# A list scheduler that knows PSUM banks, for a two-layer hybrid decoder trunk

## The chip, the cores and the metric

The kernel runs on one core of one Trainium2 chip. The metric is device time of one execution in microseconds (us). Three executions of the kernel before took 213.7, 214.15 and 214.66 us, with a median of 214.15.

## The reference

The reference takes a residual stream x of 256 rows by 1024 columns through two layers and a last RMSNorm, all in float32. Cut to what matters:

```
h = x
hn = rmsnorm(h, norm_gain[0])                      # layer 0: hn @ w_in (2832 columns)
  A: gated linear attention, 4 heads, chunks of 64, low-rank decay;  rmsnorm * silu(a_gate)
  B: sliding-window attention (128), 8 heads, 2 kv heads, sinks;     * silu(b_gate)
h = h + concat(A, B) @ w_out_even
hn = rmsnorm(h, norm_gain[1])                      # layer 1: hn @ w_in (2560 columns)
  C: causal attention over one block of 256, 8 heads, 2 kv heads;    * silu(c_gate)
h = h + C @ w_out_odd
out = h * rsqrt(mean(h * h) + 1e-6) * final_gain
```

With 256 rows there is one block of 256, so the block selection of branch C picks nothing and only a query's own causal block counts.

## The kernel before

The rows are two tiles (t = 0, 1) of 128; the 1024 model columns are eight tiles k of 128. Every large product is made of three fast matmuls: each operand is split into a rounded part ("h", as wh, xh, ogh) and a residual ("l", as wl, xl, ogl), and `products` (L381) adds h*h, l*h and h*l into one PSUM bank.

Weights come in chunks of 512 KB. `load_w` (L333) records for each chunk a DMA on SP's queue into one of four "raw" buffers, a rounding to wh (ScalarE or VectorE, whichever the planner picks) and a residual wl on VectorE. A fifth load has to wait until the raw buffer of the first has been read by both.

PSUM has eight banks of 128x512 float32: four "pj" for projections, two "s" for scores and transposes, one "t" for transposes, one "o" for attention outputs. `bank` (L317) hands them out in turn.

The work is first recorded and then issued. Each call on an engine goes through `Plan.record` (L156), which makes a node with its engine, a cost in ns, its dependences and the label of its section. `copy` (L75) makes a node that ScalarE or VectorE may do. `Plan.order` (L213) is a list scheduler: it keeps a clock for each engine, takes for each the candidate of the highest rank that is ready at the earliest time, and issues the one that starts first. A rank is the length of the path to the end plus numbers from the table `BOOST` (L278), one for each label and one for each label and engine. SP's loads keep the order in which they were recorded. Each engine then runs its list in that order, and semaphores keep the dependences.

Two places matter for the change. In the handover between the layers (L838 to L853) the residual sum h1 is made in five pieces (t = 0: two of 512 columns; t = 1: 512, 256, 256); each is transposed into an "s" bank in 128-wide blocks, and `split` (L376) turns every block into xh (a `copy`) and xl (VectorE, from the same bank and xh). In the tail (L907 to L932) the same five pieces of the last sum are added, squared and summed, multiplied by the final gain and scaled: the first piece of a tile is squared on ScalarE, the others on VectorE by one instruction that also adds to the sum so far; POOL takes the power -1/2; VectorE then scales 720 columns and ScalarE 304, and SP's and ScalarE's queues write them out.

Of the kernel before, what the change touches and what calls it, by code (L numbers as in the profile page):

```python
# [11 lines left out]
F32 = mybir.dt.float32  # L12
# [3 lines left out]
AF = mybir.ActivationFunctionType  # L16
# [33 lines left out]
class Plan:  # L50
# [12 lines left out]

    class Node:
        __slots__ = ("eng", "forms", "cost", "tail", "deps", "users", "path", "left", "ready", "end", "table", "dma", "idx", "load", "boost", "label",
                     "tag", "start", "rank")

    def __init__(self, nc):
        self.nodes, self.access, self.boost, self.label = [], {}, 0.0, "start"
# [86 lines left out]
    def record(self, eng, real, method, args, kw):  # L156
        if self.joined:
            node = self.joined[0]
            emit = node.forms[eng][2]
            node.forms = {eng: (node.cost, node.tail, lambda: (emit(), getattr(real, method)(*args, **kw)))}  # L160
            self.depend(node, args[:1], args[1:])
# [12 lines left out]
        node.boost = self.boost  # L174
        node.label = self.label
        (node.cost, node.tail), node.table, node.dma = self.cost(eng, method, out, args, kw), None, 0
        node.load = False
        node.forms = {eng: (node.cost, node.tail, lambda: getattr(real, method)(*args, **kw))}  # L178
        if eng == "ACT" and method == "activation":
            node.table = self.TABLE.get(args[2])  # L180
        if method == "dma_start":
            n = 4
            for _, c in list(out.ap):
                n *= c
            node.dma, node.load = n, "DRam" in type(args[1].tensor).__name__
        self.depend(node, outs, ins)

    def depend(self, node, outs, ins):
# [24 lines left out]
    def order(self):  # L213
# [8 lines left out]
        clock = dict.fromkeys(self.ENGINES, 800.0)  # L222
        cand = {e: [] for e in self.ENGINES}
        table, dma = None, 0.0
        for n in nodes:
            n.left, n.ready = len(n.deps), 0.0
            if not n.left:
                for e in n.forms:
                    cand[e].append(n)
        result, queue = [], [n.idx for n in nodes if n.eng == "SP"]  # L230
        while len(result) < len(nodes):
            best = None
            for e, c in cand.items():
                if e == "SP":
                    c = [n for n in c if n.idx == queue[0]] if queue else []
                if not c:
                    continue
                first = max(clock[e], min(n.ready for n in c))
                pick = max((n for n in c if n.ready <= first),
                           key=lambda n: n.rank - (PENALTY if n.table and n.table != table else 0))  # L240
                if best is None or (first, first + pick.forms[e][0]) < (best[0], best[0] + best[1].forms[best[2]][0]):
                    best = (first, pick, e)
            start, n, n.eng = best
            for e in n.forms:
                cand[e].remove(n)
            if n.eng == "SP":
                queue.pop(0)
            cost, tail, _ = n.forms[n.eng]
            if n.eng == "PE" and start < COLD:
                cost *= 1.85  # L250
            if n.table and n.table != table:
                table, cost = n.table, cost + 1283
            end = start + cost
            n.start = start
            clock[n.eng] = end
            if n.dma:
                dma = max(dma, start + (1500 if n.eng != "POOL" else 2500)) + n.dma / 400.0
                tail = dma + 500 + LATE - end
            result.append(n)
            for u in n.users:  # L260
                u.left -= 1
                u.ready = max(u.ready, end + 2 if u.eng == n.eng == "PE" else end + tail + self.latency(n, u))
                if not u.left:
                    for e in u.forms:
                        cand[e].append(u)
            n.end = end + tail
        self.span = max(n.end for n in nodes)
        return result

# [5 lines left out]
SIZE = {F32: 4, F32R: 4, BF16: 2, I8: 1}  # L275


BOOST = {"start": 98597, "start.DVE": 3254, "start.ACT": 96019, "start.PE": -31948, "rstd": 31475, "rstd.ACT": -37, "rstd.POOL": -24983, "rstd.PE": -12434, "bk": 36804, "bk.PE": 217, "bk.DVE": -81736, "bq": 3171, "bq.PE": 3109, "bq.DVE": -20905, "decay": 21203, "decay.PE": 74853, "decay.ACT": 3469, "decay.DVE": -187598, "bg": 11332, "bg.ACT": -33239, "bg.DVE": -731, "bg.PE": 899, "swa0": -12879, "swa0.PE": 10779, "swa0.POOL": -36260, "swa0.DVE": 45500, "swa0.ACT": 97090, "aq": -302768, "aq.ACT": -7847, "aq.DVE": -24230, "aq.PE": 7553, "ak": 6472, "ak.ACT": 904, "ak.DVE": -359375, "ak.PE": -179473, "swa1": -53249, "swa1.PE": 51429, "swa1.POOL": 127883, "swa1.DVE": -83638, "swa1.ACT": -185141, "gla": -44871, "gla.PE": 1809, "gla.ACT": 8127, "gla.DVE": 17088, "gla.POOL": -46, "ag": -382194, "ag.ACT": -117298, "ag.DVE": 4974, "ag.PE": -81161, "agate": 103853, "agate.ACT": -15208, "agate.PE": 106711, "oe": -565024, "oe.ACT": -6313, "oe.DVE": 33451, "oe.PE": -60361, "h1": -30627, "h1.DVE": 34676, "h1.PE": -40731, "h1.ACT": 94131, "h1.POOL": -72111, "odd": -133964, "odd.PE": 80018, "odd.DVE": -32828, "cv": 86415, "cv.DVE": -91321, "cv.PE": -14630, "ck": 5306, "ck.ACT": 54210, "ck.DVE": 16958, "ck.PE": -1368074, "q0": -42079, "q0.ACT": -37389, "q0.DVE": 81387, "q0.PE": -77423, "g0": 86994, "g0.ACT": 50548, "g0.DVE": 25243, "g0.PE": 146202, "moba0": 44850, "moba0.PE": 4255, "moba0.DVE": -5618, "moba0.ACT": 21294, "q1": -4528, "q1.ACT": -120247, "q1.DVE": 2101, "q1.PE": 54307, "g1": 25170, "g1.ACT": -104958, "g1.DVE": -60832, "g1.PE": -10042, "moba1": 165732, "moba1.PE": 38343, "moba1.ACT": -291161, "oo": -273149, "oo.ACT": -7130, "oo.DVE": -150278, "tail.DVE": 38832, "tail.ACT": -123887, "tail.POOL": -155413, "tail.SP": 30960}  # L278
COLD = 6500
WARM = 7  # L280
PENALTY, LATE = 12000, 600


@with_exitstack
def trunk(ctx: ExitStack, tc: tile.TileContext, t_in, out):
# [621 lines left out]
    nc.label = "tail"  # L907
    for t in range(NT):
        e = ends if t else (0, 512, D)
        y, r = xr[:, t], rstd[2][:, t:t + 1]  # L910
        total = buf("tot", [P, 1], F32, 4)
        for i, (lo, hi) in enumerate(zip(e, e[1:])):
            sl = slice(lo, hi)
            nc.vector.tensor_add(h1[:, t, sl], o[t, lo, hi], h1[:, t, sl])
            part_mean = ssq[:, 4 + 4 * t + i:5 + 4 * t + i]
            if i == 0:
                nc.scalar.activation(buf("junk", [P, D], BF16)[:, sl], h1[:, t, sl], AF.Square, scale=D ** -0.5,
                                     accum_out=part_mean)
# [77 lines left out]
```

## Time and profile before

The profiled execution is one further run, with the profiler's records.

| what | value |
|---|---|
| profiled execution's own time | 215.43 us |
| its span, first to last instruction | 213.7 us |
| median of three runs | 214.15 us |
| TensorE busy | 202.4 us, 95% |
| VectorE busy | 172.5 us, 81% |
| ScalarE busy | 109.3 us, 51% |
| GpSimd busy | 12.9 us, 6% |
| mean granted TensorE clock | 0.995 |
| read from HBM | 34.76 MB, 168 GB/s over the span |

A busy time is the sum of an engine's instructions, so overlaps with other engines are not taken off, and the ends of matmuls are modelled. The page also has a chain of work that ended last, followed back from the last instruction: 80% of it is TensorE, 6% VectorE, 5% DMA.

### The profile page before, as it was taken

What the parts mean: (1) busy time and instruction counts of PE and PEld (TensorE: products, weight loads), DVE (VectorE), ACT (ScalarE), POOL (GpSimd) and SP (SyncE); (2) the same over time, 40 slices, a digit from 0 to 9 for tenths busy, and PEclk for the clock granted to TensorE, in tenths of its full rate; (3) what the DMA queues carried; (4) which work ended last, traced back from release to release, by engine and by line L of the source; (5) the groups of instructions that cost most, each with busy time, mean ns of one, the idle gap of its engine ahead of it and who ended that gap; (6) DMA issues with size and microseconds to landing.
All of it is one profiled execution on the core that took longest, in us unless ns stands there. A gap on an engine that the chain in (4) does not pass through costs nothing.

```text
span 213.7 us, 3783 instructions
## 1 busy us (share of the span) xinstructions
PE 202.4 (95%) x1431; PEld 183.8 (86%) x1431; DVE 172.5 (81%) x358; ACT 109.3 (51%) x215; POOL 12.9 (6%) x38
## 2 busy tenths in 40 slices
PE   7899999999999999999898999999999999999970
PEld 3799999998898777888697999999999999888860
DVE  4699979998999998684578985876899998975662
ACT  3365857985998356611327500433868792613011
POOL 6005000010000000210001010000000000000101
PEclk9999999999999999999999999999999999999997
DMA  6999987673433094272027753157870019020022
GB/s 185 369 406 346 362 330 207 222 263 101 146 148 101 11 376 139 46 233 84 0 80 251 250 214 98 23 210 273 284 259 38 0 37 338 23 96 3 0 98 98
DMA packets 10913, 36.05 MB, mean 169 GB/s; under 512 B 1344, under 2 KB 2064, under 8 KB 10896
## 3 DMA queue, kind: packets, MB, share of 16 engines
q1 hardware_dynamic: 10464, 35.34, 48.0%
q10 hardware_dynamic: 432, 0.48, 0.6%
q8 instruction: 11, 0.18, 0.3%
q14 instruction: 6, 0.05, 0.1%
HBM read 34.76 MB, written 1.05 MB: 168 GB/s over the span
## 4 chain that ended last, share of the span: by engine, by line
PE 80%; DVE 6%; DMA 5%; issue 3%; ACT 2%; SPq 1%; POOL 0%; POOLq 0%; ACTq 0%; DVEq 0%
PE pj L178 61%; PE s L178 8%; PE o L178 7%; PE t L178 3%; DMA raw<-in_q 3%; DMA raw<-in_xav 3%; DVE xh L82 1%; PE s L160 1%; DVE xl L178 1%; DVE wl L178 1%; DVE wh L82 1%; ACT xh L178 1%; DVE xt L178 1%; SPq L178 1%; ACT wh L178 1%
## 5 line engine op out<-in xcount | busy, mean ns | idle before, releaser
L178 DVE TENSOR_TENSOR wl<-raw,wh 128x1024 fp32r<-128x1024 f32 (+2 forms) x59 | 68.5, 1170 | 2.9 <-ACT wh L178 1.8
L178 PE MATMUL pj<-xh,wh 128*128 128x256 f32 x224 | 54.9, 291 | 0.4 <-ACT wh L178 0.3
L178 PE MATMUL pj<-xh,wl 128*128 128x256 f32 x224 | 53.7, 288 | 0.0
L178 PE MATMUL pj<-xl,wh 128*128 128x256 f32 x224 | 53.6, 287 | 0.0
L178 ACT ACTIVATE wh<-raw 128x1024 fp32r<-128x1024 f32 (+2 forms) x36 | 36.5, 1016 | 32.3 <-PE pj L178 10.9
L178 PEld LDWEIGHTS pj<-xh,wh 128*128 128x128 f32 x224 | 38.5, 191 | 1.1 <-ACT wh L178 0.8
L178 PEld LDWEIGHTS pj<-xh,wl 128*128 128x128 f32 x224 | 38.4, 192 | 0.4 <-issue 0.3
L178 PEld LDWEIGHTS pj<-xl,wh 128*128 128x128 f32 x224 | 38.2, 191 | 0.2
L82 DVE CAST wh<-raw 128x1024 fp32r<-128x1024 f32 (+2 forms) x23 | 15.5, 672 | 16.9 <-PE pj L178 8.7
L178 PE MATMUL pj<-wl,ogh 128*128 128x512 f32 (+1 forms) x64 | 21.8, 376 | 0.0
L178 PE MATMUL pj<-wh,ogh 128*128 128x512 f32 (+1 forms) x64 | 21.6, 374 | 0.0
L178 PE MATMUL pj<-wh,ogl 128*128 128x512 f32 (+1 forms) x64 | 21.5, 374 | 0.0
L178 PE MATMUL pj<-wh,xl 128*128 128x328 f32 (+2 forms) x64 | 17.8, 348 | 1.9 <-DVE xl L178 1.9
L178 PE MATMUL pj<-wh,xh 128*128 128x328 f32 (+2 forms) x64 | 18.7, 357 | 0.7 <-ACT xh L178 0.4
L178 PE MATMUL pj<-wl,xh 128*128 128x328 f32 (+2 forms) x64 | 17.1, 333 | 0.0
L178 ACT ACTIVATE prob<-neg,mn 128x129 f32<-128x129 f32 (+3 forms) x32 | 14.2, 445 | 1.7 <-DVE mn L178 1.5
L178 PEld LDWEIGHTS pj<-wh,xl 128*128 128x128 f32 x64 | 11.6, 197 | 3.2 <-DVE xl L178 2.8
L178 PEld LDWEIGHTS pj<-wh,xh 128*128 128x128 f32 x64 | 11.5, 197 | 2.8 <-ACT xh L178 0.9
L178 PEld LDWEIGHTS pj<-wh,ogl 128*128 128x128 f32 x64 | 12.0, 189 | 1.9
L178 PEld LDWEIGHTS pj<-wl,ogh 128*128 128x128 f32 x64 | 11.9, 188 | 2.0 <-DVE wl L178 0.2
L178 PEld LDWEIGHTS pj<-wh,ogh 128*128 128x128 f32 x64 | 11.8, 188 | 1.8
L178 PE MATMUL t<-ident,prob 128*128 128x128 f32 x48 | 12.5, 276 | 0.0
(186 smaller groups left out, 338.1 us busy)
## 6 DMA issues: line engine op xcount, KB each, us to landing
raw<-in_oe SPq DMA_DIRECT2D x8, 512.0 KB, 4.2
raw<-in_q SPq DMA_DIRECT2D x8, 512.0 KB, 4.9
raw<-in_g SPq DMA_DIRECT2D x8, 512.0 KB, 4.5
raw<-in_oo SPq DMA_DIRECT2D x8, 512.0 KB, 4.2
raw<-in_bq SPq DMA_DIRECT2D x4, 512.0 KB, 6.4
raw<-in_bg SPq DMA_DIRECT2D x4, 512.0 KB, 5.5
raw<-in_ag SPq DMA_DIRECT2D x4, 512.0 KB, 3.8
raw<-in_xav SPq DMA_DIRECT2D x4, 456.0 KB, 6.5
```

The source lines that it names most:

```text
L82: lambda: getattr(self.vector._real, name)(*args, **kw))
L160: node.forms = {eng: (node.cost, node.tail, lambda: (emit(), getattr(real, method)(*args, **kw)))}
L178: node.forms = {eng: (node.cost, node.tail, lambda: getattr(real, method)(*args, **kw))}
```

## The change

Four things change. Each node gets a list of the PSUM banks it touches (`banks`). The scheduler's `order` remembers for every bank until when each engine uses it, and counts a node as ready only when the other engines' uses have ended (plus a hand-over latency). An engine other than SP may now be kept waiting for up to `LOOK` = 130 ns for a node whose rank is higher by more than `MARGIN` = 1500. The table `BOOST` has new numbers throughout. And the tail is written otherwise: every piece but a tile's last is squared on ScalarE and its sum added on by a one-column VectorE addition; only a tile's first 512 columns are multiplied by the gain ahead of the power, and the other 512 are multiplied by power and gain in one VectorE instruction; each output queue now takes 512 columns.

```diff
@@ record
+        node.banks = sorted({x.tensor.name for x in outs + ins if "PSUM" in str(getattr(x.tensor, "space", ""))})
@@ order
+        bank = {}
+
+        def ready(n, e):
+            return max([n.ready] + [t + self.latency(n, n) for b in n.banks for o, t in bank.get(b, {}).items() if o != e])
...
-                first = max(clock[e], min(n.ready for n in c))
-                pick = max((n for n in c if n.ready <= first),
-                           key=lambda n: n.rank - (PENALTY if n.table and n.table != table else 0))
+                when = {n.idx: ready(n, e) for n in c}
+                first = max(clock[e], min(when.values()))
+
+                def gain(n):
+                    return n.rank - (PENALTY if n.table and n.table != table else 0)
+
+                pick = max((n for n in c if when[n.idx] <= first), key=gain)
+
+                soon = [n for n in c if first < when[n.idx] <= first + LOOK and n.rank > gain(pick) + MARGIN]
+                if soon and e != "SP":
+                    pick = max(soon, key=lambda n: n.rank)
+                    first = when[pick.idx]
...
+            for b in n.banks:
+                bank.setdefault(b, {})[n.eng] = max(n.end, bank.get(b, {}).get(n.eng, 0.0))
@@ constants
-BOOST = {"start": 98597, "start.DVE": 3254, ...}
+BOOST = {"start": 308260, "start.DVE": -15127, ... "bq.DVE": -722225, ... "agate.DVE": -729706, ...}
-PENALTY, LATE = 12000, 600
+PENALTY, LATE, LOOK, MARGIN = 12000, 600, 130, 1500
@@ tail
-        y, r = xr[:, t], rstd[2][:, t:t + 1]
-        total = buf("tot", [P, 1], F32, 4)
+        y, r, mean = xr[:, t], rstd[2][:, t:t + 1], EPS
         for i, (lo, hi) in enumerate(zip(e, e[1:])):
             sl = slice(lo, hi)
             nc.vector.tensor_add(h1[:, t, sl], o[t, lo, hi], h1[:, t, sl])
             part_mean = ssq[:, 4 + 4 * t + i:5 + 4 * t + i]
-            if i == 0:
+            if hi < D:
                 nc.scalar.activation(buf("junk", [P, D], BF16)[:, sl], h1[:, t, sl], AF.Square, scale=D ** -0.5,
                                      accum_out=part_mean)
-                nc.vector.tensor_scalar(total, part_mean, EPS, None, op0=ALU.add)
+                total = buf("tot", [P, 1], F32, 4)
+                nc.vector.tensor_scalar(total, part_mean, mean, None, op0=ALU.add)
+                mean = total
             else:
                 nc.vector.tensor_tensor_reduce(out=buf("junk", [P, hi - lo]), in0=h1[:, t, sl], in1=h1[:, t, sl],
-                                               op0=ALU.mult, op1=ALU.add, scale=1.0 / D, scalar=total,
+                                               op0=ALU.mult, op1=ALU.add, scale=1.0 / D, scalar=mean,
                                                accum_out=part_mean)
-                total = part_mean
-            nc.boost = -2000.0
-            nc.vector.tensor_mul(y[:, sl], h1[:, t, sl], fg[lo // 512][:, lo % 512:hi - lo // 512 * 512])
-            nc.boost = 0.0
-        nc.gpsimd.tensor_tensor(r, total, half_neg[:, 0:1], op=ALU.pow)
-        nc.vector.tensor_scalar(y[:, 0:720], y[:, 0:720], r, None, op0=ALU.mult)
-        nc.sync.dma_start(out[t * P:(t + 1) * P, 0:720], y[:, 0:720])
-        nc.scalar.activation(y[:, 720:D], y[:, 720:D], AF.Copy, scale=r)
-        nc.scalar.dma_start(out[t * P:(t + 1) * P, 720:D], y[:, 720:D])
+            if i == 0:
+                nc.vector.tensor_mul(y[:, sl], h1[:, t, sl], fg[0])
+        nc.gpsimd.tensor_tensor(r, part_mean, half_neg[:, 0:1], op=ALU.pow)
+        nc.vector.scalar_tensor_tensor(y[:, 512:D], h1[:, t, 512:D], r, fg[1], op0=ALU.mult, op1=ALU.mult)
+        nc.sync.dma_start(out[t * P:(t + 1) * P, 512:D], y[:, 512:D])
+        nc.scalar.activation(y[:, 0:512], y[:, 0:512], AF.Copy, scale=r)
+        nc.scalar.dma_start(out[t * P:(t + 1) * P, 0:512], y[:, 0:512])
```

## Rows read from the trace of the kernel before

**Rows 1.** The page: busy us (share of span) x instructions of each engine.

```profile
PE 202.4 (95%) x1431; PEld 183.8 (86%) x1431; DVE 172.5 (81%) x358; ACT 109.3 (51%) x215; POOL 12.9 (6%) x38
```

**Rows 2.** Waits of TensorE (us in total, times, longest); last row 6 to 12 us.

```profile
PE pj L178 <- DVE xl L178: 1.9, 3, 0.7
...
PE o L178 <- ACT junk L178: 0.5, 1, 0.5
PE pj L178 <- ACT xh L178: 0.4, 1, 0.4
PE pj L178 <- ACT wh L178: 0.3, 1, 0.3
PE pj L178 <- DVE xt L178: 0.2, 1, 0.2
...
PE pj L178 <- DVE xl L178: 0.6, 1, 0.6
```

**Rows 3.** Timeline, 100 to 121 us: start, us, engine, operation, [idle before <-releaser].

```profile
101.61 0.37 ACT L178 ACTIVATE xh<-s,xt 128x128 fp32r<-128x128 f32 x1 [1.01 <-PE s L178]
...
102.02 0.35 DVE L82 TENSOR_SCALAR xh<-s,xt 128x128 fp32r<-128x128 f32 x1 [0.75 <-ACT xh L178]
...
103.07 1.12 DVE L178 SCALAR_TENSOR_TENSOR xl<-s,xt,xh 128x128 fp32r<-128x128 f32 x4
103.47 0.39 PE L178 MATMUL pj<-wh,xl 128*128 128x256 f32 x1 [0.58 <-DVE xl L178]
...
110.09 0.87 DVE L82 TENSOR_SCALAR xh<-s,xt 128x128 fp32r<-128x128 f32 x3 [0.38 <-ACT xh L178]
```

**Rows 4.** Waits of VectorE and of ScalarE for each other.

```profile
DVE xh L82 <- ACT xh L178: 2.3, 5, 0.8
...
ACT junk L178 <- DVE oa L82: 1.0, 1, 1.0
```

**Rows 5.** Chain of waits (start, us, what), 0 to 10 and 138 to 150 us.

```profile
7.79 0.84 DVE wl L178
...
139.83 1.14 DVE wl L178
...
141.37 6.16 DMA raw<-in_q
...
148.75 1.34 PE pj L178 x9
```

**Rows 6.** Timeline of the tail, 195 us to the end.

```profile
205.13 0.63 ACT L178 ACTIVATE junk<-xt 128x512 bf16<-128x512 f32 x1 [1.83 <-DVE xt L178]
...
205.67 0.19 ACT L178 ACTIVATION_READ_ACCUMULATOR junk<-xt 128x1 f32 x1
...
205.89 0.16 DVE L178 TENSOR_SCALAR tot<-ssq 128x1 f32<-128x1 f32 x1
...
206.86 0.28 PE L178 MATMUL o<-wl,ogh 128*128 128x256 f32 x1
207.05 0.48 DVE L178 CUSTOM_DVE_ANT_0 junk<-xt,tot 128x256 f32<-128x256 f32 x1
...
207.46 0.42 DVE L178 TENSOR_TENSOR xt<-o,xt 128x256 f32<-128x256 f32 x1
...
208.13 0.48 DVE L178 CUSTOM_DVE_ANT_0 junk<-xt,ssq 128x256 f32<-128x256 f32 x1
...
208.53 0.42 DVE L178 TENSOR_TENSOR xr<-xt,va 128x256 f32<-128x256 f32 x1
208.69 0.66 POOL L178 TENSOR_TENSOR rstd<-ssq,half_neg 128x1 f32<-128x1 f32 x1 [5.97 <-DVE ssq L178]
...
209.39 0.60 DVE L178 TENSOR_SCALAR xr<-xr,rstd 128x720 f32<-128x720 f32 x1 [0.44 <-POOL rstd L178]
```

**Rows 7.** Groups by form (xcount | busy us, mean ns | idle); last: POOL's timeline.

```profile
L178 DVE TENSOR_TENSOR wl<-raw,wh 128x1024 fp32r<-128x1024 f32 x53 | 64.2, 1220 | 2.8 <-ACT wh L178 1.8 <-PE pj L178 0.4
...
L178 DVE SCALAR_TENSOR_TENSOR ogl<-t,small,ogh 128x512 fp32r<-128x512 f32 x2 | 1.5, 748 | 0.4 <-ACT ogh L178 0.4
...
124.40 0.56 POOL L178 TENSOR_TENSOR rstd<-rsq,half_neg 128x1 f32<-128x1 f32 x1 [9.74 <-DVE rsq L178]
```

More of the change, by code (lines that the diff above doesn't have):

```diff
@@ L65 @@
         __slots__ = ("eng", "forms", "cost", "tail", "deps", "users", "path", "left", "ready", "end", "table", "dma", "idx", "load", "boost", "label",
-                     "tag", "start", "rank")
+                     "tag", "start", "rank", "banks")
     def __init__(self, nc):
@@ L160, in record @@
             node.forms = {eng: (node.cost, node.tail, lambda: (emit(), getattr(real, method)(*args, **kw)))}
+            node.banks = sorted({*node.banks, args[0].tensor.name})
             self.depend(node, args[:1], args[1:])
@@ L275 @@
 SIZE = {F32: 4, F32R: 4, BF16: 2, I8: 1}
-BOOST = {"start": 98597, "start.DVE": 3254, "start.ACT": 96019, "start.PE": -31948, "rstd": 31475, "rstd.ACT": -37, "rstd.POOL": -24983, "rstd.PE": -12434, "bk": 36804, "bk.PE": 217, "bk.DVE": -81736, "bq": 3171, "bq.PE": 3109, "bq.DVE": -20905, "decay": 21203, "decay.PE": 74853, "decay.ACT": 3469, "decay.DVE": -187598, "bg": 11332, "bg.ACT": -33239, "bg.DVE": -731, "bg.PE": 899, "swa0": -12879, "swa0.PE": 10779, "swa0.POOL": -36260, "swa0.DVE": 45500, "swa0.ACT": 97090, "aq": -302768, "aq.ACT": -7847, "aq.DVE": -24230, "aq.PE": 7553, "ak": 6472, "ak.ACT": 904, "ak.DVE": -359375, "ak.PE": -179473, "swa1": -53249, "swa1.PE": 51429, "swa1.POOL": 127883, "swa1.DVE": -83638, "swa1.ACT": -185141, "gla": -44871, "gla.PE": 1809, "gla.ACT": 8127, "gla.DVE": 17088, "gla.POOL": -46, "ag": -382194, "ag.ACT": -117298, "ag.DVE": 4974, "ag.PE": -81161, "agate": 103853, "agate.ACT": -15208, "agate.PE": 106711, "oe": -565024, "oe.ACT": -6313, "oe.DVE": 33451, "oe.PE": -60361, "h1": -30627, "h1.DVE": 34676, "h1.PE": -40731, "h1.ACT": 94131, "h1.POOL": -72111, "odd": -133964, "odd.PE": 80018, "odd.DVE": -32828, "cv": 86415, "cv.DVE": -91321, "cv.PE": -14630, "ck": 5306, "ck.ACT": 54210, "ck.DVE": 16958, "ck.PE": -1368074, "q0": -42079, "q0.ACT": -37389, "q0.DVE": 81387, "q0.PE": -77423, "g0": 86994, "g0.ACT": 50548, "g0.DVE": 25243, "g0.PE": 146202, "moba0": 44850, "moba0.PE": 4255, "moba0.DVE": -5618, "moba0.ACT": 21294, "q1": -4528, "q1.ACT": -120247, "q1.DVE": 2101, "q1.PE": 54307, "g1": 25170, "g1.ACT": -104958, "g1.DVE": -60832, "g1.PE": -10042, "moba1": 165732, "moba1.PE": 38343, "moba1.ACT": -291161, "oo": -273149, "oo.ACT": -7130, "oo.DVE": -150278, "tail.DVE": 38832, "tail.ACT": -123887, "tail.POOL": -155413, "tail.SP": 30960}
@@ new lines @@
+BOOST = {"start": 308260, "start.DVE": -15127, "start.POOL": 192, "start.ACT": 38547, "start.PE": -17663, "rstd": -19560, "rstd.ACT": 124955, "rstd.DVE": 115059, "rstd.POOL": -55563, "rstd.PE": -2940, "bk": 72927, "bk.PE": 5299, "bk.DVE": 11568, "bq": 7879, "bq.PE": -45059, "bq.DVE": -722225, "decay": 9816, "decay.PE": 6603, "decay.ACT": -500, "decay.DVE": 38759, "bg": -20668, "bg.ACT": 103347, "bg.DVE": 117872, "bg.PE": 64, "swa0": 19, "swa0.PE": -69516, "swa0.POOL": -109470, "swa0.DVE": -7370, "swa0.ACT": 282880, "aq": -181490, "aq.ACT": 4177, "aq.DVE": 60141, "aq.PE": 92879, "ak": 8425, "ak.ACT": -29078, "ak.DVE": -348491, "ak.PE": -362233, "swa1": -149581, "swa1.PE": -165615, "swa1.POOL": 19736, "swa1.DVE": 102002, "swa1.ACT": 306, "gla": -284590, "gla.PE": -120020, "gla.ACT": 42214, "gla.DVE": -71418, "ag": -374820, "ag.ACT": -22320, "ag.DVE": 335720, "ag.PE": -25022, "agate": 695074, "agate.ACT": 63820, "agate.DVE": -729706, "agate.PE": -71178, "oe": -546740, "oe.ACT": -89986, "oe.DVE": 195978, "oe.PE": 569, "h1": -81572, "h1.DVE": -112059, "h1.PE": 12477, "h1.ACT": -13693, "h1.POOL": 52549, "odd": 61629, "odd.PE": 41833, "odd.DVE": 22886, "cv": 183952, "cv.ACT": 16099, "cv.DVE": 16721, "cv.PE": -3543, "ck": -713826, "ck.ACT": 36419, "ck.DVE": 70132, "ck.PE": 92, "q0": 144341, "q0.ACT": -335824, "q0.DVE": 113390, "q0.PE": -39462, "g0": 15555, "g0.ACT": 29812, "g0.DVE": 4814, "g0.PE": -592, "moba0": -16830, "moba0.PE": 27130, "moba0.DVE": 310737, "moba0.ACT": 18881, "q1": 9659, "q1.ACT": -62076, "q1.DVE": -24498, "q1.PE": 767, "g1": 5202, "g1.ACT": 23863, "g1.DVE": -102820, "g1.PE": 3052, "moba1": -5391, "moba1.PE": 13736, "moba1.DVE": 5712, "moba1.ACT": -93948, "oo": -386614, "oo.ACT": 8440, "oo.PE": 16538, "tail": -83075, "tail.DVE": -60119, "tail.ACT": 22636, "tail.SP": 74670}
```

## The prediction, made before the changed kernel ran

> **What bounds the kernel now.** I read the page's busy times first [rows 1]. TensorE is busy for 202.4 us or 95% of the span, VectorE for 172.5 and ScalarE for 109.3. TensorE therefore sets the time: a new order of work can win only what TensorE loses in the fill at the start, between its matmuls, and behind its last one.
>
> Second, the waits of TensorE [rows 2], which are what an order can remove. They add up to 3.3 us: 1.9 for a residual part xl of the normalized operand (three times), 0.5 for a square on ScalarE, 0.4 for a rounded part xh, 0.3 for rounded weights wh, 0.2 for the residual stream. The same view of 6 to 12 us has one of the waits for xl, 0.6, and the wait for xh, 0.4: those are the fill. The other two waits for xl (0.58 at 103.47 [rows 3] and the longest, 0.7; together 1.3) are in the handover from layer one to layer two.
>
> Third, what stands before those waits, in order of time [rows 3]. Four pieces of one transposed bank "s" are rounded to xh, one on ScalarE at 101.61, the next on VectorE at 102.02, and so on by turns. They read different columns and write different columns, yet VectorE's piece has an idle 0.75 us before it that ends with ScalarE's piece. The list of waits says how much of that there is [rows 4]: VectorE waits 2.3 us in 5 places for ScalarE's xh. ScalarE's square of the branch output also waits 1.0 us for VectorE's scaled copy of the same bank, though neither needs the other's result. So two engines never read a PSUM bank together here, and the old planner, which knows no such rule, handed alternate pieces to two engines as if they ran side by side. This is the error that the change corrects.
>
> Behind TensorE's last matmul lie 6.6 us [rows 6]: it ends at 207.14 (206.86 and 0.28), the span at 213.7.
>
> **The change part by part.**
>
> *Bank knowledge.* It adds no instruction; it changes the times that the planner reckons with, and so who takes a piece and when. Price of the alternation: from the first xh at 101.61 to the start of the residuals at 103.07 are 1.46 us for four pieces [rows 3]. The same work on one engine: three pieces on VectorE took 0.87 us, so a further piece costs (0.87 - 0.35) / 2 = 0.26, and four take 0.35 + 3 x 0.26 = 1.13. That saves 0.33 us in each chain that alternates. The two handover waits of 1.3 us hang on such chains. Lower bound 0.66 (the faster chain alone), upper 1.3 (the planner, which now sees the chain at its true length, also places enough other matmuls beside it). I take 1.0, between the two, since TensorE has matmuls of both layers on hand at this point (the output product of one, the first projection of the next) and the planner can see that it lacks 0.3 us more.
>
> The 0.5 us behind the square: the two reads of the bank stay in line whoever does them, so the wait goes only if other matmuls are put there. Between 0 and 0.5; I take 0.2, nearer the lower end because the reads don't shorten.
>
> The remaining 0.3 for wh and 0.2 for the residual stream come from a DMA's landing and an addition, on which bank knowledge has no hold: 0. The fill: its 0.6 and 0.4 may shrink or grow by about as much when the start gets new priorities (the first chain runs through a DMA that no priority hastens): 0, with 0.6 either way.
>
> *Short looks ahead.* An engine may now stand idle for up to 130 ns when clearly more urgent work is about to be ready. SP is excepted. Queued behind the work so preferred is whatever else the engine had ready, a weight split above all, whose residual takes 1.22 us on VectorE [rows 7]. VectorE is idle for 41 us in all (213.7 - 172.5), so 0.13 us at a time is covered unless it falls where a split is late; I take 0, with the bad end in the rival below.
>
> *New priorities.* These reorder everything, and no row prices them directly. Bounds: a gain of at most what TensorE waits, 3.3 us; a loss of one or two late weight splits, priced below. I take 0 beyond the terms above.
>
> *Final scaling.* Before, after the last matmul [rows 6]: VectorE sums the squares of piece two (207.05, 0.48), only then adds piece three (207.46, 0.42, although TensorE was done at 207.14), multiplies piece two by the gain, sums piece three's squares (208.13), POOL takes the power (208.69, 0.66), VectorE scales 720 columns (209.39, 0.60), and 3.71 us after the end of that scaling (209.99) the span is over. After: piece two's squares go to ScalarE, and the gain of the upper half moves into the last scaling. VectorE is then free at 207.05, so the addition of piece three can start at 207.2 and end at 207.6. The sum that its square-sum needs is now a chain ScalarE to VectorE: for the 512-wide piece the square started at 205.13, its sum was out at 205.86 (205.67 and 0.19), and the one-column addition ended at 206.05 (205.89 and 0.16) [rows 6]: 0.92 us, the upper bound for 256 columns, so 207.05 + 0.92 = 207.97. With the 128-wide ScalarE piece's 0.37 [rows 3] in place of the 512-wide square's 0.63 it is 207.71, the lower bound. I take 207.85 for the square-sum's start, between the two as 256 lies between 128 and 512, 0.28 before 208.13: the wait for ScalarE takes the place of the removed multiplication, and wins a little.
>
> The power: 0.66 with a VectorE multiplication of two SBUF operands running beside it at 208.53, 0.56 alone, in the layer before [rows 6, 7]. After the change nothing of VectorE runs beside it: 0.10 gained. The Trainium skill (SBUF — State Buffer, Who interferes with whom) says that a VectorE instruction with two SBUF inputs contends with a GpSimd instruction that reads SBUF. The trace agrees with it by these two durations; without that rule the 0.10 would be chance, and the tail's gain 0.13 in place of 0.23.
>
> The last scaling now multiplies by a column and a second tensor: the nearest row, 128x512 with a column and a second tensor, took 0.748 against 0.60 for the 720 columns [rows 6, 7]: a loss of 0.15. ScalarE's part grows from 304 to 512 columns, by the square of that width 0.63 [rows 6], so it ends before VectorE does. The two output DMAs carry the same bytes in all, split evenly; they overlap already, so 0.
>
> Tail: 0.28 + 0.10 - 0.15 = 0.23 gained; between 0 and 0.5, as the last square is early or late.
>
> *Sum.* 1.0 + 0.2 + 0.23 = 1.4 us. The profiled execution took 215.43 us (span 213.7 and 1.7 around it), 1.28 above the median of the runs, 214.15. So 214.0 on the profiled execution's scale, and 212.7 as a median.
>
> **The rivals.**
>
> *More than the handover gains.* With a true picture of the banks, the new priorities also remove the waits that I left: all 3.3 us and the tail's 0.23, or 214.15 - 3.5 = 210.6. For: none of the waits is in TensorE's own work, and the fill's chain puts a weight residual of 0.84 us [rows 5] ahead of the operand that TensorE waits for, which an order can turn round. Against: the fill and the wait for wh hang on DMAs.
>
> *No change.* The banks' turns remain, since one bank is read by one engine at a time whatever the planner knows; if the handover has no more matmuls to put beside the chain, its waits move to a neighbouring place and only the tail's gain shows: 213.9. For: 95% of the span is TensorE's work, which stays. Against: the four xh alone are 0.33 us shorter on one engine, twice.
>
> *Slower: a weight split comes late.* SP issues loads in a fixed order, each when a raw buffer is free, that is, after the split of the chunk four earlier. In the chain of waits a residual runs at 139.83; after its end at 140.97 come SP's issue, a DMA of 6.16 us and a rounding on ScalarE, and TensorE starts at 148.75, having waited for that rounding [rows 2, 5]: 7.8 us from split to matmul, with nothing to spare. New priorities that put such a split behind one more residual and one 512-wide product of VectorE (1.22 + 0.75 [rows 7]) delay TensorE by 2.0 there. It decides as soon as a split ends less than 7.8 us before its buffer's next chunk is due. One such place, with the handover unimproved and the tail's gain, gives 214.15 + 2.0 - 0.23 = 215.9. For: the split labels' priorities are moved by hundreds of thousands, more than the length of the whole kernel in ns, so the paths' lengths alone no longer keep them in order. Against: the planner counts loads and buffers, so it sees most of this.
>
> That the change doesn't do what it says would be seen as an xh chain that still alternates; its time is that of no change.
>
> **How the numbers follow.** The forecast, 212.7, has 0.40; the larger gain, 210.6, 0.21; no change, 213.9, 0.23; slower, 215.9, 0.16. Within 0.5% (213.1 to 215.2) is about what a measurement of this kernel can't tell from no change. Faster: the first two, 0.40 + 0.21 = 0.61; same 0.23; slower 0.16. The forecast's own range, by the lower and upper terms (0.66 + 0 + 0 and 1.3 + 0.5 + 0.5, and half of the fill's 0.6 either way), is 211.5 to 213.8. For eight in ten the range reaches down to the larger gain and up to the edge of the slower case: 210.2 to 215.5.
>
> **What would show it.** Right: the wait of VectorE's xh for ScalarE's xh falls from 2.3 to under 0.5 us; TensorE's waits for xl after 10 us fall under 0.4; TensorE's last matmul ends at about 206.0 on the profiled scale; the last square-sum starts 0.7 us after TensorE's end in place of 1.0; the power takes about 0.56, the last scaling 0.75. Wrong: the handover's waits return as waits for another operand, or waits for wh or wl of over 1 us appear. A span in which TensorE ends earlier by more than 2 us would mean that the waits listed here were not all that the order cost.

## The result, and the profile after

The changed kernel takes 215.85 us (median of 17 runs, 214.8 to 217.49). The kernel before took 214.54 in 17 runs beside them. The ratio is 1.007, with a 95% interval of 1.0049 to 1.0091: slower by 0.7%, and outside the predicted range.

The profiled execution of the changed kernel took 217.33 us with a span of 215.6. That is 1.5 above its own median, where the profiled execution of before lies 0.9 above its own (215.43 against 214.54), so 0.6 of the 1.9 us between the two spans is scatter of single executions.

The page's line of busy times comes first, as in [rows 1].

```profile
PE 204.9 (95%) x1431; PEld 183.2 (85%) x1431; DVE 174.0 (81%) x358; ACT 111.4 (52%) x215; POOL 13.8 (6%) x38
```

TensorE runs the same 1431 matmuls as before, yet is busy for 204.9 us in place of 202.4. The overlap of one matmul with the next is counted once in this number (before, a matmul of 512 columns is listed with 0.39 us while the next starts 0.23 us after it, at 99.57 and 99.80), so a row of matmuls that is broken up by short stalls appears here as a busier engine. Next, the waits of TensorE, which answer to [rows 2] (us in total, times, longest; a wait for the warm-up at the start, the same in every kernel here, is left out).

```profile
...
PE s L179 <- DVE xt L179: 0.9, 1, 0.9
PE pj L179 <- DVE xl L179: 0.6, 1, 0.6
PE o L179 <- ACT ad L179: 0.6, 1, 0.6
PE pj L179 <- ACT wh L179: 0.3, 1, 0.3
PE o L179 <- DVE pTh L82: 0.3, 1, 0.3
```

The two handover waits for xl are gone: the 0.6 that is left is the fill. In their place stands one wait of 0.9 for the residual stream xt. The list is even shorter than before, 2.7 us against 3.3, and still TensorE ends at 209.35 in place of 207.14: the list alone would have given the wrong sign.

VectorE's waits (same columns) show what changed for it. The wait of its own xh pieces for ScalarE's, 2.3 us [rows 4], is not there any more. What it waits 1.9 us for, once, is a bank whose four xh ScalarE has all made, and which its residual xl needs. Its residuals wl now wait 7.3 us for the rounded weights, where they waited 1.8 [rows 7].

```profile
DVE wl L179 <- ACT wh L179: 7.3, 6, 2.0
...
DVE xl L179 <- ACT xh L179: 1.9, 1, 1.9
```

The timeline of the handover, 100 to 106 us, answers to [rows 3] (start, us, engine, operation, idle before and its releaser).

```profile
100.25 1.06 ACT L179 ACTIVATE wh<-raw 128x1024 fp32r<-128x1024 f32 x1 [4.31 <-DMA raw<-in_cv]
...
101.34 1.22 DVE L179 TENSOR_TENSOR wl<-raw,wh 128x1024 fp32r<-128x1024 f32 x1 [2.04 <-ACT wh L179]
...
102.48 0.74 DVE L179 SCALAR_TENSOR_TENSOR ogl<-t,small,ogh 128x512 fp32r<-128x512 f32 x1
...
103.15 1.21 DVE L179 TENSOR_TENSOR wl<-raw,wh 128x1024 fp32r<-128x1024 f32 x1
...
104.28 0.68 DVE L179 TENSOR_TENSOR xt<-pj,xr 128x512 f32<-128x512 f32 x1
...
105.02 0.66 PE L179 MATMUL s<-ident,xt 128*128 128x128 f32 x4 [0.87 <-DVE xt L179]
```

VectorE stands idle for 2.04 us at the head of its queue, with a residual whose weight chunk of branch C has landed late. Behind it in the same queue wait a residual of the gated output (ogl), one more weight residual and only then the first addition of h1, for whose transposes TensorE is waiting.

The chain of waits (start, us, what) shows the same place and the one that the slower rival had named [rows 5].

```profile
89.14 2.28 DVE wl L179 x2
...
92.85 7.32 DMA raw<-in_cv
100.25 1.07 ACT wh L179
...
104.36 0.61 DVE xt L179
105.02 0.66 PE s L179 x4
...
140.94 1.24 DVE wl L179
142.57 6.48 DMA raw<-in_q
149.16 1.07 ACT wh L179
150.27 1.22 PE pj L179 x8
```

By the page, VectorE now holds 20% of this chain and DMAs 15%, where it was 6% and 5% before; TensorE holds 52% in place of 80%. At 140 to 150 us the chain of [rows 5] runs as before. The chunk that lands late is one of in_cv, whose loads left SP from 92.85 on, behind two residuals of VectorE. Before, they left from 89.10 on:

```profile
89.10 0.85 SPq L178 DMA_DIRECT2D raw<-in_cv  x2
```

Last, the tail, which answers to [rows 6] (timeline, 208.4 us to the end).

```profile
208.43 0.42 ACT L179 ACTIVATE junk<-xt 128x256 bf16<-128x256 f32 x1 [1.77 <-DVE xt L179]
...
209.07 0.28 PE L179 MATMUL o<-wl,ogh 128*128 128x256 f32 x1
209.39 0.42 DVE L179 TENSOR_TENSOR xt<-o,xt 128x256 f32<-128x256 f32 x1 [0.20 <-PE o L179]
209.85 0.48 DVE L179 CUSTOM_DVE_ANT_0 junk<-xt,tot 128x256 f32<-128x256 f32 x1
...
210.42 0.54 POOL L179 TENSOR_TENSOR rstd<-ssq,half_neg 128x1 f32<-128x1 f32 x1 [7.29 <-DVE ssq L179]
...
211.00 0.75 DVE L179 SCALAR_TENSOR_TENSOR xr<-xt,rstd,va 128x512 f32<-128x512 f32 x1 [0.66 <-POOL rstd L179]
```

TensorE is done at 209.35 (209.07 and 0.28) and the span at 215.6: 6.25 us, against 6.56 before (213.7 - 207.14).

### The profile page after: what moved, and what is told of

Same layout as the page of the kernel before. It is cut to its first block, busy times and chain, and to the rows that moved or that the text cites. A ratio compares the mean times of both kernels' runs of the same rounds, so it can differ in the third digit from the quotient of the medians.

```text
span 215.6 us, 3774 instructions
## 1 busy us (share of the span) xinstructions
PE 204.9 (95%) x1431; PEld 183.2 (85%) x1431; DVE 174.0 (81%) x358; ACT 111.4 (52%) x215; POOL 13.8 (6%) x38
## 4 chain that ended last, share of the span: by engine, by line
PE 52%; DVE 20%; DMA 15%; issue 5%; ACT 4%; SPq 1%; POOL 1%; POOLq 0%; ACTq 0%; DVEq 0%
PE pj L179 40%; DVE wl L179 7%; PE s L179 5%; PE o L179 4%; DMA xr<-in_xr 4%; DMA raw<-in_cv 3%; DMA raw<-in_q 3%; DMA raw<-in_bq 3%; PE t L179 2%; DVE neg L179 2%; DVE og L179 2%; ACT wh L179 1%; ACT prob L179 1%; DMA raw<-in_av 1%; DVE am L179 1%
## 5 line engine op out<-in xcount | busy, mean ns | idle before, releaser
L179 PE MATMUL pj<-xh,wh 128*128 128x256 f32 x224 | 56.6, 289 | 0.3 <-ACT wh L179 0.3
L179 ACT ACTIVATE wh<-raw 128x1024 fp32r<-128x1024 f32 (+2 forms) x38 | 38.6, 1017 | 34.5 <-DMA raw<-in_q 11.6
L179 PE MATMUL pj<-xh,wl 128*128 128x256 f32 x224 | 55.7, 287 | 0.0
L179 PE MATMUL pj<-xl,wh 128*128 128x256 f32 x224 | 55.4, 286 | 0.0
L179 PEld LDWEIGHTS pj<-xh,wh 128*128 128x128 f32 x224 | 39.5, 191 | 1.3 <-ACT wh L179 0.7
L179 PEld LDWEIGHTS pj<-xh,wl 128*128 128x128 f32 x224 | 39.4, 191 | 0.7 <-DVE wl L179 0.2
L179 PEld LDWEIGHTS pj<-xl,wh 128*128 128x128 f32 x224 | 39.3, 191 | 0.1
L82 DVE CAST wh<-raw 128x1024 fp32r<-128x1024 f32 (+2 forms) x21 | 14.0, 666 | 15.4 <-PE pj L179 3.4
L179 PE MATMUL pj<-wh,ogl 128*128 128x512 f32 (+1 forms) x64 | 22.9, 372 | 0.0
L179 PE MATMUL pj<-wh,xh 128*128 128x328 f32 (+2 forms) x64 | 17.6, 342 | 0.1
```

Of the source, the lines that this page charges most:

```text
L82: lambda: getattr(self.vector._real, name)(*args, **kw))
```

## The experiments

Each ratio is to the kernel before, run beside it on the same chip, with its 95% interval. "Old table" means the numbers of `BOOST` before, "banks" the bank knowledge, "look" the short looks ahead.

**The tail by itself, put in and taken out.** tail_only is the kernel before with the new tail; tail_undone is the changed kernel with the old one.

```diff
-        nc.vector.tensor_scalar(y[:, 0:720], y[:, 0:720], r, None, op0=ALU.mult)
+        nc.vector.scalar_tensor_tensor(y[:, 512:D], h1[:, t, 512:D], r, fg[1], op0=ALU.mult, op1=ALU.mult)
...
```

> The old planner with its old priorities, and only the new tail. Theory (the loss lies in the new order of work, the tail gains): TensorE's end stays within 0.3 us of before's 207.1, the stretch behind it shrinks from 6.58 to about 6.25 us, as in the changed kernel, so 0.3 us faster than before, ratio about 0.9985. Rival (the new tail is the loss): over 1 us slower than before.

> The changed kernel with the old tail put back. Theory: 0.3 us slower than the changed kernel, so about 1.6 us slower than before (ratio about 1.008), with TensorE's end at about 209.3. Rival (the tail is the loss): back to before's time.

tail_only: 214.4 us, 0.9974 (0.9954 to 0.9994), a gain of 0.1 to 1.0 us. tail_undone: 216.02 us, 1.0044 (1.0019 to 1.007), which can't be told from the changed kernel's 1.007. Neither expectation came true as written: in tail_only's profile TensorE ends at 206.03, 1.1 us earlier than before and not within 0.3, and tail_undone is not slower than the changed kernel. The traces show why. With the old order the stretch behind TensorE shrinks from 6.56 to 6.37 us (212.4 - 206.03). With the changed kernel's order the old tail already needs only 6.13 (214.2 - 208.07), less than the new one's 6.25. TensorE's last matmul and the last square-sum of tail_undone are:

```profile
207.79 0.28 PE L179 MATMUL o<-wl,ogh 128*128 128x256 f32 x1
...
208.57 0.48 DVE L179 CUSTOM_DVE_ANT_0 junk<-xt,ssq 128x256 f32<-128x256 f32 x1
```

So the tail is worth a few tenths with the old order and shows no gain with the new one, and it is not what made the changed kernel slower.

**The banks by themselves, and the alternation by itself.** bank_only has the new `ready` and the new `banks`, with the old table, the old tail and no look (first fence, as against the changed kernel; its table and tail are those of before). xh_one_engine replays the order of before from a written list and only gives the alternating xh pieces to VectorE (second fence, shortened: in the code the list is packed).

```diff
-PENALTY, LATE, LOOK, MARGIN = 12000, 600, 130, 1500
+PENALTY, LATE, LOOK, MARGIN = 12000, 600, -1, 1500
```

```diff
-        for n in self.order():
-            n.forms[n.eng][2]()
+        for i, e in WRITTEN:
+            self.nodes[i].forms[e][2]()
```

> Old priorities, old tail, no look ahead; the scheduler only learns the banks. Theory of the prediction, first half (bank knowledge gains at the handover): the alternating xh go to one engine in pairs, VectorE's waits for ScalarE's xh fall from 2.3 to under 0.5 us, TensorE's handover waits for xl from 1.3 to 0.6 or less, and the time by 0.7 to 1.3 us (ratio 0.994 to 0.997). Rival (the chain was hidden or its waits only move): within 0.3 us of before. Second rival (bank knowledge makes the order worse, as in the changed kernel): over 0.5 us slower.

> Before's order, written down and replayed instruction by instruction, with one difference: the eight xh pieces of the first bank of each row tile in the handover, which alternate between ScalarE and VectorE, all go to VectorE. Theory: each of the two chains is 0.33 us or more shorter and TensorE's two waits for xl (0.58 and 0.7) shrink by about that, 0.4 to 0.9 us faster in all. Rival (other work on VectorE takes the gain back, since VectorE now has four more pieces of 0.35 us): within 0.3 us of before.

bank_only: 212.09 us, 0.986 (0.9831 to 0.989), 3.0 us faster and more than either theory gave. xh_one_engine: 213.86 us, 0.995 (0.9932 to 0.9969), 1.1 us faster (0.7 to 1.5), within the 0.66 to 1.3 that the prediction had worked out for the handover and a little over the 0.4 to 0.9 expected of this run. TensorE runs the same list here as before, so its two handover waits can be set side by side: they fall from 0.58 [rows 3] and 0.69 (first line) to 0.18 and 0.28, by 0.8 us in all.

```profile
116.12 0.39 PE L178 MATMUL pj<-wh,xl 128*128 128x256 f32 x1 [0.69 <-DVE xl L178]
```

```profile
102.37 0.39 PE L181 MATMUL pj<-wh,xl 128*128 128x256 f32 x1 [0.18 <-DVE xl L181]
...
114.70 0.39 PE L181 MATMUL pj<-wh,xl 128*128 128x256 f32 x1 [0.28 <-DVE xl L181]
```

The other 1.9 us of bank_only are left for all else that the planner arranges anew; no run takes them apart. The timelines of the handover show how the xh are now done: ScalarE takes all four in bank_only (first fence), VectorE in xh_one_engine (second).

```profile
101.15 1.14 ACT L179 ACTIVATE xh<-s,xt 128x128 fp32r<-128x128 f32 x4 [1.00 <-PE s L179]
```

```profile
100.94 1.12 DVE L85 TENSOR_SCALAR xh<-s,xt 128x128 fp32r<-128x128 f32 x4 [0.35 <-PE s L181]
```

Four pieces take 1.12 to 1.14 us on one engine (1.13 by the prediction), and 1.46 by turns [rows 3]. The Trainium skill (PSUM — Partial Sum Buffer, PSUM bank collisions raise a hardware error) asks software to guard PSUM by bank, reads against reads too; the idle 0.75 us of [rows 3] and its going away agree.

**Each new part taken out of the changed kernel.** numbers_undone has the old table, look_off no look, bank_off ignores the banks.

```diff
# bank_off
-            return max([n.ready] + [t + self.latency(n, n) for b in n.banks for o, t in bank.get(b, {}).items() if o != e])
+            return n.ready
```

> The changed kernel with the old priority table alone put back; banks, look ahead and tail stay new. Theory (the old table was fitted to a scheduler without a look; a look of 130 ns reorders its close decisions): clearly slower than the changed kernel, by several us, ratio to before 1.02 or more, so that the new table repairs what the look breaks. Rival (the new table by itself is the loss): about as fast as bank knowledge with the new tail, ratio about 0.984.

> The changed kernel with the look ahead alone switched off; banks, new table and tail stay. Theory (the new table is fitted to the look): slower than the changed kernel by 1 to 3 us, ratio to before 1.012 to 1.022. Rival (the look is the loss, whatever the table): faster than the changed kernel, at or under before's time.

> The changed kernel with bank knowledge alone switched off; look, new table and tail stay. Theory (bank knowledge is a gain wherever it stands): slower than the changed kernel by 2 to 5 us, ratio to before over 1.016, and VectorE again waits over 1 us for ScalarE's reads of the same bank. Rival (the bank rule is over-careful with this table): no slower than the changed kernel.

numbers_undone: 226.23 us, 1.0536 (1.0503 to 1.0568). look_off: 222.4, 1.0351 (1.0317 to 1.0386). bank_off: 225.08, 1.0461 (1.0431 to 1.0491). numbers_undone and bank_off came out as the theory said (in bank_off VectorE's xh wait 3.9 us for ScalarE's again); look_off lies above its 1.012 to 1.022. None of the three can be taken out by itself without a loss of 2.8% or more. In two of them a part of the loss is TensorE's clock, which stays at 1.00 up to TensorE's end in the profiles of all the other kernels. The lines give a stretch of time, its length, the busy us and instructions of PE, PEld, DVE, ACT and POOL, the granted clock, the DMAs' share and GB/s (look_off first, bank_off second):

```profile
80.00:90.00 10.00, 7.12 (x51) 4.45 (x50) 9.49 (x18) 5.11 (x8) 0.00 (x0) 0.97 0.30 106
90.00:100.00 10.00, 9.44 (x44) 8.39 (x45) 5.26 (x12) 3.68 (x7) 1.02 (x1) 0.69 0.25 80
```

```profile
100.00:110.00 10.00, 8.09 (x38) 6.91 (x36) 6.66 (x9) 1.07 (x2) 0.00 (x0) 0.83 0.61 238
```

In look_off TensorE waits several times between 85 and 91 us, and from 90 to 96 us the granted clock is 0.50, the lower of its two levels (1.2 GHz). In bank_off a wait of 1.9 us ends at 103.72, and at 105 to 107 us the clock is 0.50. By the shares of clock that are missing, this took at most 3.4 us in look_off and 1.7 in bank_off (estimates from these lines: 0.03 and 0.31 of 10 us, 0.17 of 10 us). By that estimate look_off would stand near 1.02 at the full clock, still slower than the changed kernel. So the new table holds only for the rules that it was found with, and with the old table the look costs 7% (1.0536 against the 0.9855 of the next run).

**The banks and the tail together.** bank_and_tail is the changed kernel without the look and with the old table.

> Old priorities, bank knowledge, new tail, no look ahead: the changed kernel without its new priorities and its look ahead. Theory (bank knowledge and tail each gain and add up; the priorities with the look lose it): the gains measured alone, 1.4% and 0.26%, add to about 1.7%, ratio 0.982 to 0.986, and TensorE's end stays at about 204. Rival (the tail's gain needs slack that bank knowledge has used up): ratio 0.986, as with bank knowledge alone.

It takes 211.93 us, 0.9855 (0.9831 to 0.988): the best of all, 1.5% faster than before, though within the noise no better than bank_only. Its page and its waits of TensorE:

```profile
PE 201.0 (96%) x1431; PEld 183.3 (87%) x1431; DVE 170.3 (81%) x349; ACT 109.7 (52%) x222; POOL 12.7 (6%) x38
```

```profile
...
PE pj L179 <- DVE xl L179: 0.6, 1, 0.6
PE pj L179 <- ACT wh L179: 0.2, 1, 0.2
```

TensorE ends at 203.19, 6.2 us before the changed kernel's. Of these, 1.9 are listed waits (2.7 less 0.8) and 3.9 lie inside its busy time (204.9 less 201.0). The 6.2 us are of two single executions, one 1.5 us above its median and one 0.7 below (211.27 against 211.93); by the ratios, 1.007 and 0.9855, the distance is 2.2%, some 4.6 us.

**Whose look it is.** On top of bank_and_tail, the look for TensorE only, and for the three other engines only; and the changed kernel with the look for all but TensorE.

```diff
-                if soon and e != "SP":
+                if soon and e in ("PE",):                  # look_TensorE
+                if soon and e in ("ACT", "DVE", "POOL"):   # look_others, look_spares_TensorE
```

> Old priorities, banks and new tail, and the look ahead for TensorE alone. Theory (TensorE's look is what costs: its next matmul of the same accumulation is ready 2 ns after the last one by the planner's reckoning, so the look makes TensorE stay with one accumulation or one row of transposes where it took turns before): most of the 6.7% that the look cost with the old table (1.0536 against 0.9855) comes from here, ratio to before 1.03 to 1.055, and TensorE's 80 transposes no longer stand singly. Rival (the look of VectorE and ScalarE costs, since it idles them 0.13 us at a time): ratio 0.985 to 1.0.

> Old priorities, banks and new tail, and the look ahead for ScalarE, VectorE and GpSimd but not for TensorE. Theory (TensorE's look is what costs): at most a third of the 6.7%, ratio to before 0.985 to 1.005, all 80 transposes single. Rival (VectorE's look costs): 1.03 or more.

> The changed kernel, table and all, with the one difference that TensorE has no look ahead. Theory (the new table was fitted to TensorE's look, and has repaired most of what it costs): near the changed kernel, ratio to before 0.99 to 1.012, not the 0.985 of the old table with banks, since the table no longer fits. Rival (the look is a loss under any table): 0.99 or less.

look_TensorE: 222.82 us, 1.0377 (1.0341 to 1.0414). look_others: 216.96, 1.0096 (1.0063 to 1.0128). Against 0.9855 that is 5.3% and 2.4%, so TensorE's look costs the most under the old table, and the others' is not free: look_others is above the theory's 1.005 and under the rival's 1.03. look_spares_TensorE: 217.38, 1.012 (1.0079 to 1.0161): with the new table TensorE's look may stay or go. The page and TensorE's waits of look_TensorE:

```profile
PE 207.6 (94%) x1431; PEld 183.7 (83%) x1431; DVE 172.7 (78%) x356; ACT 110.0 (50%) x217; POOL 12.8 (6%) x38
```

```profile
PE pj L179 <- DVE xl L179: 1.7, 2, 1.1
...
PE pj L179 <- ACT xh L179: 1.1, 1, 1.1
PE pj L179 <- DVE wl L179: 0.8, 2, 0.5
PE pj L179 <- DVE wh L82: 0.7, 1, 0.7
```

There is no single place: beside bank_and_tail the listed waits grow at operands of all kinds, and TensorE's busy time by 6.6 us.

**Long or short.** The look of TensorE cut to 10 ns, and to what lies between 10 and 130 ns, each on top of bank_and_tail.

```diff
-                soon = [n for n in c if first < when[n.idx] <= first + LOOK and n.rank > gain(pick) + MARGIN]
+                soon = [n for n in c if first + 10 < when[n.idx] <= first + LOOK and n.rank > gain(pick) + MARGIN]   # look_long
```

> Old table, banks, new tail, and for TensorE alone a look of 10 ns: it can only hold TensorE to the accumulation it is in, whose next matmul is ready 2 ns later by the planner's reckoning. Theory (staying with one accumulation is what costs): most of the 5.2% of TensorE's look, ratio to before 1.02 or more, transposes in rows. Rival (the true waits cost): 0.985 to 1.005.

> Old table, banks, new tail, and for TensorE alone a look that begins at 10 ns: only true waits of 10 to 130 ns, with the turns between accumulations kept. Theory (staying with one accumulation is what costs): 0.985 to 1.01, transposes single. Rival (the true waits cost): 1.02 or more.

look_short: 217.4 us, 1.011 (1.0068 to 1.0151). look_long: 217.87, 1.013 (1.0073 to 1.0187). They cost 2.6% and 2.8% beyond bank_and_tail, where the theory and its rival each put the loss in one of the two. So it does not follow how long TensorE may be kept idle, which points to the order that comes out, though no run shows that by itself. In look_long 72 of the 80 transposes stand singly and in look_short 25 (counted in the traces), so the rows of transposes that the theory had named don't tell the two apart.

**Other tables.** refound is bank_and_tail with numbers found anew by a random search that keeps what shortens the planner's own reckoning. refit_others starts that search from the new table, without TensorE's look; refit_all from the new table with all rules.

> Banks and new tail without a look, with a priority table found anew by a random search of my own over the planner's reckoned span, started from the old table. Theory (finding priorities anew is no loss in itself; the old table with banks stands near the floor): within 0.5% of the old table with banks and tail, ratio to before 0.981 to 0.990. Rival (tables fitted to the planner's reckoning do worse on the chip): 0.995 or more.

> The changed kernel, but TensorE has no look ahead, and the table is fitted anew to that rule by my own random search over the planner's reckoned span, started from the changed kernel's table. Theory (TensorE's look costs under any table): as the table of the run refound, ratio to before 0.985 to 0.998, at least 1% under the changed kernel, with most of the 80 transposes single. Rival (a table fitted to the look loses nothing by it; the loss is that searched tables do worse on the chip): no better than the changed kernel, 1.004 or more.

> The changed kernel with its rules whole, TensorE's look included, and the table fitted on from the changed kernel's by the same search for as long. Theory: the search finds no way round TensorE's look, so the time stays with the changed kernel's, ratio to before 1.003 to 1.012. Rival (the changed kernel's table was simply not fitted far enough): 0.998 or less.

refound: 213.28 us, 0.9928 (0.99 to 0.9955), which is worse than the old table it started from. refit_others: 217.4, 1.0104 (1.0057 to 1.015). refit_all: 217.61, 1.0103 (1.006 to 1.0146). The theory that TensorE's look is what keeps the changed kernel slow fell with refit_others, which has no such look and a table fitted on to its rules; there the rival held (1.004 or more). For refound neither held: it lies between the theory's 0.990 and the rival's 0.995. refit_all is where its theory put it. A table fitted further to the planner's picture gave no gain on the chip in any of the three.

**One instruction at the handover.** h1_first replays the changed kernel's order from a written list, and moves one instruction on VectorE: the residual that stood idle at 101.34 goes behind the addition of h1. All other engines' orders are the same.

```diff
 # VectorE's list
-wl<-raw,wh
 ogl<-t,small,ogh
 wl<-raw,wh
 xt<-pj,xr
+wl<-raw,wh
```

> The changed kernel's order, written down and replayed, with one VectorE instruction moved: the residual of the second cv weight chunk, for whose rounding VectorE stands idle for 2.04 us at 99.3, goes behind the first addition of the handover, 23 places later in the list (and with it the load that reuses its buffer). Theory (VectorE's queue order makes the handover's wait): VectorE's 2.04 us of idle time there go, the first h1 addition starts 1 to 2 us earlier, TensorE's wait of 0.9 for it goes, and the time falls by 0.5 to 1.5 us against the changed kernel, ratio to before 0.999 to 1.005. Rival (TensorE then waits for the moved residual itself, or for the load behind it): no faster than the changed kernel, 1.006 or more.

h1_first: 214.88 us, 1.0002 (0.9981 to 1.0022), against 1.007 for the changed kernel: 0.7%, about 1.5 us (0.8 to 2.1), from one place in a queue, as the theory said. Its timeline and TensorE's waits:

```profile
101.19 1.23 DVE L182 TENSOR_TENSOR wl<-raw,wh 128x1024 fp32r<-128x1024 f32 x1 [1.40 <-PE o L182]
...
103.02 0.69 DVE L182 TENSOR_TENSOR xt<-pj,xr 128x512 f32<-128x512 f32 x1 [0.60 <-PE pj L182]
103.62 1.22 DVE L182 TENSOR_TENSOR wl<-raw,wh 128x1024 fp32r<-128x1024 f32 x1
103.76 0.42 PEld L182 LDWEIGHTS s<-ident,xt 128*128 128x128 f32 x4 [0.30 <-DVE xt L182]
```

```profile
...
PE pj L182 <- ACT xh L182: 0.7, 1, 0.7
PE pj L182 <- DVE xl L182: 0.6, 1, 0.6
PE s L182 <- DVE qT L182: 0.3, 1, 0.3
PE o L182 <- DVE pTh L85: 0.2, 1, 0.2
```

The addition now starts when its product is ready, at 103.02 in place of 104.28, the transposes start 1.26 us earlier (103.76 and 105.02), and the wait for xt is gone from the list. Of the 1.26 us this execution had 0.27 before the moved place (the transposes of oa start at 97.50 and 97.77), so the move is worth 1.0 there. Another 0.7 us come at 149 to 153 us, where the wait of 0.3 for rounded weights is gone too; whether the move does that is not shown.

## Why the prediction was wrong

*Bank knowledge: the mechanism was right, the size too small.* The alternation went away, and its price was right: 1.0 forecast for the handover, 1.1 measured in xh_one_engine, and 0.8 off its two listed waits. But the part as a whole, put at 1.0 + 0.2, is worth 3.0 us in bank_only. The prediction had bounded it by the waits that the list shows. TensorE's end moved by 3.1 us there (207.14 to 204.03), which the prediction had named as the sign that the listed waits were not all that the order cost. Of the 3.1, 1.9 are listed waits (3.3 less 1.4, with the 0.5 behind the square gone whole where 0.2 was taken) and 1.1 lie inside TensorE's busy time (202.4 less 201.3), which the prediction had priced at nothing. So the sum was wrong on both sides, and the two errors partly cancel: bank knowledge was worth 1.8 us more than forecast, the next two parts cost 4.6 more.

*Short looks ahead, "I take 0": failed.* The argument was that VectorE is idle for 41 us, which covers 0.13 us at a time. It priced the idle time alone. But under the old table the look costs 5.3% for TensorE alone and 2.4% for the others alone, and one of only 10 ns on TensorE still costs 2.6%: its price is not the time stood idle.

*New priorities, "I take 0": failed.* Its bounds, plus 3.3 and minus one or two late splits, were too narrow at the bad end. With banks and new tail in place, the four cases are: old table without a look 0.9855, old table with it 1.0536, new table without it 1.0351 (a part of that the clock), new table with it 1.007. So either of the two by itself costs more than both. The new table is worth 4.7 points with the look (1.0536 to 1.007), yet the pair of look and table together costs 2.2% against the old table without a look (1.007 against 0.9855): some 4.6 us of 214.5. That pair turned a gain of 3 us into a loss of 1.3. The prediction had treated the two as separate edits with one answer; they can only be priced as a pair.

*Final scaling: right for the old order, right by luck for the changed kernel.* Forecast 0.23. With the old order the stretch behind TensorE shrinks by 0.19 (tail_only, 6.56 to 6.37); the runs alone, 0.26% or 0.6 us (0.1 to 1.0), are too coarse to tell. In the changed kernel it shrinks by 0.31, but not by the forecast steps. The last square-sum starts 0.50 us after TensorE's end (forecast 0.7, before 1.0), and it does so with the old tail in the new order too (tail_undone, 208.57 and 208.07): the new order makes that gain, not the new tail. The power takes 0.54 (0.56; before 0.66) and the last scaling 0.75 (0.75), as forecast. From the end of the last scaling to the end of the span it is 3.85 us in place of 3.71 (215.6 - 211.75, 213.7 - 209.99; in tail_only 3.85 too), where the prediction had put the output DMAs at 0. The power's shorter time with nothing of VectorE beside it agrees with the rule of the Trainium skill that the prediction weighed (SBUF — State Buffer, Who interferes with whom).

*The rivals.* The slower rival, 215.9 with a chance of 0.16, comes to within 0.05 us of the measured time, and that is luck. Half of its mechanism is seen at the handover: residuals of VectorE come late, the loads behind them leave from 92.85 in place of 89.10, and a chunk lands late. But TensorE does not wait for that chunk, as the rival has it: VectorE stands idle for it, and TensorE waits for the addition queued behind. By h1_first that costs 1.5 us and not 2.0, and not at 140 us. The rival's other condition, a handover unimproved, did not hold: the alternation is gone, and what offsets that gain is spread over the whole kernel. "Waits return as waits for another operand" was the sign that the prediction had set for being wrong, and xt is that operand.

*What stays open.* Of the 2.2%, some 4.6 us, between the changed kernel and bank_and_tail, one site is settled: 1.5 us by the runs, 1.0 by the traces. The rest is not at one place, much of it lies inside TensorE's busy time, and no run tells which property of a table or of a look makes it. That the planner's picture leaves something out is likely, since searching further in that picture did not help on the chip; what it leaves out was not found.

## What to carry to other kernels

When a scheduler gets a truer model and new tuned numbers in one change, price the model with the old numbers first: here that alone was 1.4 to 1.5% faster, and the rest of the change took all of it back. Don't put a preference for urgent work or a new priority table at zero because some engine has idle time: look also at what stands behind the preferred instruction in the engine's list, above all behind one that waits for a DMA, as at the one site that was settled here. Read how many us an engine's busy time grows for the same instructions, beside its list of waits.

## What the runs showed that was not expected

- The list of waits can get shorter while the engine gets later: 2.7 us listed after against 3.3 before, with TensorE's end 2.2 us later in the profiled executions. For the same 1431 matmuls TensorE is busy for 201.0 us in bank_and_tail and for 207.6 in look_TensorE. Not all of that need be a worse order of matmuls: h1_first, where TensorE runs the changed kernel's list unaltered, is busy for 203.8 us in place of 204.9, so busy time holds stalls that the list does not.
- TensorE's transposes cost the same singly and in rows. Before, 128-wide transposes stand one by one between matmuls of 512 columns, which then start 0.35 us apart (100.29 and 100.64) in place of 0.23 (99.57 and 99.80), 0.12 each. With the look they stand in rows: after, four in a row start at 108.70, one matmul of 512 columns follows, and the next one starts at 109.39: (109.39 - 108.70 - 0.23) / 4 = 0.115 each. So the rows, though a clear mark of TensorE's look in the traces (33 of 80 single after, all 80 before), are not by themselves the loss; and look_long has the loss with few of them.
